# Later adaLN columns as sums along rows of a re-laid w_ada on VectorE, and three empty deferred jobs behind each key block

## The chip, the core and the metric

The kernel runs on one core of one Trainium2 chip. The metric is the device time of one execution in microseconds (us). The kernel before takes 1604.93 us, the median of 3 runs (1604.6 to 1605.01).

The engines are named as in the profile: PE is TensorE's matmul queue and PEld its weight loads, DVE is VectorE, ACT is ScalarE, POOL is GpSimd, SP is SyncE, which issues most of the DMAs. PSUM is the memory that TensorE writes its results to, SBUF the memory that all engines work from.

## What is computed

One trunk layer of a hybrid encoder, for a prompt of 1024 rows and a sample of 32 rows at once (1056 columns in the kernel, which keeps activations transposed, features on partitions). Each of the two has its own condition vector c (1024 values), and all of adaLN comes from it:

```python
mod = jax.nn.silu(c) @ w_ada + b_ada
sh1, sc1, gt1, sh2, sc2, gt2 = jnp.split(mod[:, None, :], 6, axis=-1)

h = rmsnorm(x, g_mix) * (1 + sc1) + sh1
u = h @ w_in
...
x = x + gt1 * (merged @ w_out)
h2 = rmsnorm(x, g_ffn) * (1 + sc2) + sh2
g, up = jnp.split(h2 @ w_gate_up, 2, axis=-1)
x = x + gt2 * ((jax.nn.silu(g) * up) @ w_down)
```

`w_ada` is 1024 x 6144 f32 (D = 1024). `sh1` and `sc1`, its first 2D columns, are needed before anything is projected. The other four vectors, columns 2D to 6D, are needed only after attention and the mLSTM. Between them, `u` is split into queries, keys and values of 8 attention heads (64 wide, in pairs `hp` of 128 partitions), the mLSTM's q, k, v and gates, and the merge gates; band softmax attention and the chunked mLSTM run on them.

## The kernel before

**Matmuls.** f32 products are made of three passes of a high and a low part (`PASSES`). A *unit* (L440) is one PSUM tile of 128 x 352: 8 steps k over the 1024 input features, 3 matmuls of 128x352 each, so 24 matmuls. A block of 128 output columns (a key block, a query block, a gate block) is three units, 72 matmuls. The class `Weights` (L55) loads raw weights ahead through SP (`wraw`, L423) and has ACT and DVE or POOL split them into high and low parts (`wsp`, L413 and L414).

**The order.** PE, ACT, DVE and POOL run in the order in which the program writes their instructions. SP's order is chosen by a scheduler, so an SP DMA can be placed elsewhere than written, but SP too issues in order. Other work is written between the matmuls of a unit by the class `Side` (L102), in two ways:

- *jobs*: generators that are stepped at every `tick` (at odd k, so four per unit), each at its own rate of steps per tick;
- *later*: a list of deferred functions; `flush(1)` takes one from the front at k = 2, 4 and 6 of each unit.

```python
            if k % 2 == 0 and k:
                side.flush(1)
            if k % 2 == 1:
                side.tick()
```

**The start.** `first_ada` (L320) makes `sh1` and `sc1` with TensorE as `w_ada`'s first 2D columns arrive; `first_units` (L471) makes the first key and value blocks of head pair 0 step by step as input rows become ready (L479). The key block (`k_block`, L548) evacuates PSUM with ACT L557 and L560 and DVE L562. The value block (`v_block`, L582) copies the value columns out of PSUM to `vf` with ACT L590 and appends to `later`: `v_tail` for the first four column blocks of 128, an empty job, `v_tail` for the other four, an empty job, and `v_sample`. `v_tail` (L608) transposes four blocks on TensorE (L615) into an `mm` PSUM tile, splits them (ACT L603, DVE L606), and the second one writes tokens out (`put_tokens`, L577, ACT L579). `v_sample` (L620) uses `sample_tail` (L569, TensorE L571, DVE L573). Then comes the query block (`q_block`, L629): three units at L447, evacuated with ACT L643 and L646. The `mm` pool has 3 PSUM buffers.

**Attention** for each of the four head pairs is a job beside the next head pair's projections. Per query block: scores on TensorE (L728) into `psS`; DVE L742 adds the bias and takes the row's extreme; ACT L743 is the exponential with a row sum; DVE L747 and POOL L748 normalise; TensorE L755 transposes into `psT`; ACT L762 copies the high part and DVE L767 makes the low part; TensorE L786 multiplies by the values into `psV`; ACT L792 and DVE L793 and L794 take it out. `psS`, `psT` and `psV` have one buffer each.

**Stretches.** `segs` (L1304) lists them: 0 the first head pair's blocks, 1 to 4 other projections with attention of head pairs 0 to 3 beside, 5 and 6 the mLSTM. At stretch 1 the job `ada_rest` (L1196) starts, 160 steps over 495 ticks, so one step in about three ticks. It computes the four later adaLN vectors without TensorE's weight path. For each of 8 chunks of 512 columns and each of 8 blocks k of 128 rows, a piece of `w_ada` (128 x 512, tile `wa`, 2 buffers, loaded by `ada_load`, L1190, DMA at L1194) is scaled by the column of silu(c) for its rows and added up:

```python
    if k == 0:
        dve.tensor_scalar(ac[:, c], wa, cmix[:, c, 0:1], None, op0=ALU.mult)
    else:
        dve.scalar_tensor_tensor(ac[:, c], wa, cmix[:, c, k:k + 1], ac[:, c],
                                 op0=ALU.mult, op1=ALU.add)
```

These are L1205 (16 times) and L1207 (112 times). The sum over the 128 rows of a block lies across partitions. So for each chunk POOL swaps the halves of the second condition (L1213, L1214), DVE adds (L1216), TensorE transposes four blocks (L1221, 32 in all), DVE reduces along the row (L1224) and adds the bias (L1225). `cmix` is silu(c) with its two conditions swapped between halves of the partitions, made by POOL in `param_cols` (L229).

Of the kernel before, what the change touches and what calls it, by code (L numbers as in the profile page):

```python
# [8 lines left out]
F32 = mybir.dt.float32  # L9
# [130 lines left out]
def hybrid_stream_step(  # L140
# [3 lines left out]
    params, w_ada, w_in, b_if, rel_row, w_br_att, w_br_mlstm, w_out, w_gate_up, w_down, g_final,  # L144
# [82 lines left out]
    cmix = cp.tile([P, 2, KD], F32, name="cmix")  # L227
# [320 lines left out]
    def k_block(hp):  # L548
        w = w_cols(KA + hp * P)

        def run():
            kt = att_k[hp] = slot([P, 2, T], F32R)
            kf = ap_.tile([P, T - 512], F32, tag="kf", name=nm("kf"), bufs=1)
            for lo, hi, pt in units(w):

                for hh, (u, v) in enumerate(ROWS):
                    act.activation(kt[u, hh, lo:hi], pt[u], AF.Copy)  # L557
                a = max(lo, 512)
                if a < hi:
                    act.activation(kf[:, a - 512:hi - 512], pt[:, a - lo:], AF.Copy)  # L560
                for hh, (u, v) in enumerate(ROWS):
                    dve.tensor_tensor(kt[v, hh, lo:hi], pt[u], f(kt[u, hh, lo:hi]), op=ALU.subtract)  # L562
            W.advance()
            sp.dma_start(new_k_p[hp], kf[:, :512])
            sp.dma_start(new_k_s[hp], kf[:, 512:])
        run.w = w
        return run

    def sample_tail(src, out, hp):  # L569
        pt = mmt()  # L570
        pe.transpose(pt[:TS, :P], src, ident)  # L571
# [259 lines left out]
    maskbig = gp.tile([P, P], F32, name="maskbig")  # L831
# [7 lines left out]
    def mlstm_setup():  # L839
        pool.memset(tri, 1.0)  # L840
        pool.affine_select(out=tri, in_=tri, compare_op=ALU.is_ge, fill=0.0, base=0,
                           pattern=[[1, P]], channel_multiplier=-1)
        pool.memset(maskbig, 0.0)
        pool.affine_select(out=maskbig, in_=maskbig, compare_op=ALU.is_ge, fill=BIG, base=0,
# [206 lines left out]
    def mlstm(pr):  # L1051
# [24 lines left out]
        def first(i):  # L1076
# [113 lines left out]
    def ada_load(n):  # L1190
        if n < 8 * KD:
            ch, k = divmod(n, KD)
            wa = ada_tiles[n] = ada_tile()
            sp.dma_start(wa, w_ada[k * P:(k + 1) * P, 2 * D + ch * 512:2 * D + (ch + 1) * 512])  # L1194

    def ada_rest():  # L1196


        for ch in range(8):
            ac = tmpt((P, 2, 512))  # L1200
            for k in range(KD):
                wa = ada_tiles.pop(ch * KD + k)
                for c in range(2):
                    if k == 0:
                        dve.tensor_scalar(ac[:, c], wa, cmix[:, c, 0:1], None, op0=ALU.mult)  # L1205
                    else:
                        dve.scalar_tensor_tensor(ac[:, c], wa, cmix[:, c, k:k + 1], ac[:, c],  # L1207
                                                 op0=ALU.mult, op1=ALU.add)
                    if c == 0:
                        ada_load(ch * KD + k + 1)  # L1210
                    yield
            swapped = ada_tile()
            pool.tensor_scalar(swapped[:DH], ac[DH:, 1], 1.0, 1.0, op0=ALU.mult, op1=ALU.mult)  # L1213
            pool.tensor_scalar(swapped[DH:], ac[:DH, 1], 1.0, 1.0, op0=ALU.mult, op1=ALU.mult)  # L1214
            yield
            dve.tensor_tensor(ac[:, 0], ac[:, 0], swapped, op=ALU.add)  # L1216
            yield
            yield
            pt = mmt()
            for j in range(4):  # L1220
                pe.transpose(pt[:, j * P:(j + 1) * P], ac[:, 0, j * P:(j + 1) * P], ident)  # L1221
            r0 = R_ADA + 2 * KD + ch * 4
            am = amod2[:, ch // 2, :, (ch % 2) * 4:(ch % 2 + 1) * 4]
            dve.tensor_reduce(am, pt.rearrange("p (k c r) -> p c k r", c=2, r=DH), mybir.AxisListType.X, ALU.add)  # L1224
            dve.tensor_tensor(am, am, cols[:, r0:r0 + 4].unsqueeze(1).to_broadcast([P, 2, 4]), op=ALU.add)  # L1225
            yield
# [3 lines left out]
    ADA_STEPS = 160  # L1230
# [61 lines left out]
    def open_mls():  # L1292
# [3 lines left out]
        mp_t.append(mls_cm)  # L1296

# [911 lines left out]
    for j in range(KD):  # L2209
# [30 lines left out]
        "params", "w_ada", "w_in", "b_if", "rel_bias",  # L2240
# [41 lines left out]
```

## Time and profile before

| | |
|---|---|
| median of 3 runs | 1604.93 us |
| the profiled execution | 1605.1 us |
| its span | 1603.4 us |
| TensorE's granted clock | full in nearly all slices of the span |
| DMA moved | 192.45 MB, 120 GB/s on the mean |

The span is the profiled execution from its first to its last instruction, without what lies around it. The profile's 40 slices show TensorE at 90% or more in all but the first two and the last:

```profile
PE   7899999999999999999999999999999999999997
DVE  7766564647776855455654699998888986799754
ACT  3556454544455544443443655544544444545443
```

Each digit is the busy share of one fortieth of the span in tenths. Such a profile is read from the engine that is always busy: the places where it stands still are few, and each has a row among its waits.

### The profile page before, as it was taken

The page shows a single profiled execution, that of the slowest core. Times are in us where ns is not written, and L with a number is a line of the kernel's source. Part 1 is how long each engine was busy: PE and PEld are TensorE (multiplying, and loading weights), DVE is VectorE, ACT ScalarE, POOL GpSimd, SP SyncE. Part 2 cuts the span into 40 slices and gives each one's busy share as a digit, 9 for nine tenths or more (in the row PEclk, how much of TensorE's full clock was granted, in tenths as well). Part 3 has the DMA queues.
Part 4 walks back from the last instruction along what each step waited for, and adds up shares of the span by engine and source line. Part 5 has one row for each costly group of instructions (what it writes and reads, how often), then busy time and mean ns, then how long its engine had stood idle before and what let it go on. Part 6 is the DMA issues. An engine that isn't in the chain of part 4 may idle for free.

```text
span 1603.4 us, 27301 instructions
## 1 busy us (share of the span) xinstructions
PE 1574.2 (98%) x10229; PEld 1554.3 (97%) x10229; DVE 1133.5 (71%) x2178; ACT 784.1 (49%) x1743; POOL 443.0 (28%) x470
## 2 busy tenths in 40 slices
PE   7899999999999999999999999999999999999997
PEld 7899999999999999999999999999999999999997
DVE  7766564647776855455654699998888986799754
ACT  3556454544455544443443655544544444545443
POOL 1334243434332411000012100565565650000001
PEclk9999999999999999999999999999999999999999
DMA  9822323232223332685353311213222227427454
GB/s 364 262 83 91 100 82 102 89 122 87 67 80 80 72 94 68 120 279 165 122 154 112 107 54 50 97 56 104 81 80 94 67 84 251 135 79 250 135 155 127
DMA packets 209362, 192.45 MB, mean 120 GB/s; under 512 B 11450, under 2 KB 179038, under 8 KB 208206
## 3 DMA queue, kind: packets, MB, share of 16 engines
q1 hardware_dynamic: 206670, 188.87, 37.9%
q8 instruction: 81, 1.33, 0.4%
q10 hardware_dynamic: 2528, 1.77, 0.4%
q14 instruction: 51, 0.42, 0.1%
q0 software_dynamic: 32, 0.06, 0.0%
HBM read 152.19 MB, written 41.63 MB: 121 GB/s over the span
## 4 chain that ended last, share of the span: by engine, by line
PE 89%; DMA 4%; DVE 3%; ACT 2%; issue 1%; SPq 0%; POOL 0%; ACTq 0%; DVEq 0%; POOLq 0%
PE mm L447 41%; PE psb L1817 18%; PE mm L1817 10%; PE mm L2220 3%; PE mm L884 3%; PE psb L2220 2%; PE psV L786 2%; PE psb L2063 2%; DMA xres<-s 1%; PE psS L728 1%; DMA s<-in_w_ada_dram 1%; PE psT L755 1%; PE mm L2063 1%; DMA wraw<-in_w_in_dram 1%; DMA s<-in_x_prompt_dram 1%
## 5 line engine op out<-in xcount | busy, mean ns | idle before, releaser
L447 PE MATMUL mm<-s,wsp 128*128 128x352 f32 x4104 | 687.8, 324 | 0.0
L447 PEld LDWEIGHTS mm<-s,wsp 128*128 128x128 f32 x4104 | 657.1, 188 | 1.5 <-issue 0.4
L414 DVE TENSOR_TENSOR wsp<-wraw,wsp 128x512 fp32r<-128x512 f32 (+1 forms) x280 | 234.9, 855 | 120.3 <-ACT wsp L413 118.7
L1817 PE MATMUL psb<-s,wsp 128*128 128x352 f32 x1611 | 271.7, 322 | 1.5 <-DVE wsp L414 0.8
L413 ACT ACTIVATE wsp<-wraw 128x512 fp32r<-128x512 f32 x336 | 199.4, 617 | 140.7 <-PE psb L1817 45.5
L1817 PEld LDWEIGHTS psb<-s,wsp 128*128 128x128 f32 x1611 | 260.5, 188 | 2.1 <-DVE wsp L414 1.1
L1817 PE MATMUL mm<-s,wsp 128*128 128x352 f32 x933 | 159.3, 322 | 0.0
L1817 PEld LDWEIGHTS mm<-s,wsp 128*128 128x128 f32 x933 | 151.2, 188 | 0.5 <-DVE wsp L414 0.5
L748 POOL TENSOR_SCALAR st<-st,mx 128x640 f32<-128x640 f32 (+5 forms) x72 | 56.1, 779 | 182.6 <-DVE mx L747 168.3
L1207 DVE SCALAR_TENSOR_TENSOR t<-wa,cmix,t 128x512 f32<-128x512 f32 x112 | 89.8, 807 | 14.3 <-DMA wa<-in_w_ada_dram 14.0
L414 POOL TENSOR_TENSOR wsp<-wraw,wsp 128x512 fp32r<-128x512 f32 x56 | 75.1, 1362 | 50.8 <-ACT wsp L413 50.3
L743 ACT ACTIVATE st<-st,mx 128x640 f32<-128x640 f32 (+5 forms) x72 | 47.9, 665 | 67.3 <-DVE mx L742 67.2
L742 DVE CUSTOM_DVE_ANT_0 st<-psS,bias 128x640 f32<-128x640 f32 (+5 forms) x72 | 44.4, 617 | 49.4 <-PE psS L728 35.2
L762 ACT ACTIVATE pT<-psT 128x640 fp32r<-128x640 f32 (+3 forms) x80 | 38.7, 494 | 64.6 <-PE psT L755 51.2
L1764 POOL TENSOR_TENSOR t<-t,sl 128x352 f32<-128x352 f32 x19 | 18.4, 969 | 182.9 <-ACT sl L1762 182.9
L2132 POOL TENSOR_TENSOR fst<-fst 128x1 f32<-128x1 f32 (+1 forms) x6 | 1.2, 194 | 236.6 <-ACT t L2125 236.6
L767 DVE TENSOR_TENSOR pT<-psT,pT 128x640 fp32r<-128x640 f32 (+3 forms) x80 | 44.0, 558 | 22.3 <-ACT pT L762 22.2
L1426 POOL TENSOR_TENSOR wraw<-wraw,raw 128x512 f32<-128x512 f32 x33 | 55.8, 1704 | 0.9
L884 PE MATMUL mm<-s,s 128*128 128x264 f32 (+3 forms) x432 | 54.7, 283 | 0.0
L2220 PE MATMUL mm<-s,wsp 128*128 128x352 f32 x330 | 54.4, 324 | 0.0
L2220 PEld LDWEIGHTS mm<-s,wsp 128*128 128x128 f32 x330 | 53.1, 188 | 0.0
L1426 POOL TENSOR_TENSOR spare<-wraw 128x512 f32<-128x512 f32 x11 | 16.8, 1527 | 130.0 <-DMA wraw<-in_w_gate_up_dram 122.2
(374 smaller groups left out, 2548.0 us busy)
## 6 DMA issues: line engine op xcount, KB each, us to landing
wraw<-in_w_in_dram SPq DMA_DIRECT2D x38, 512.0 KB, 4.3
wraw<-in_w_gate_up_dram SPq DMA_DIRECT2D x33, 512.0 KB, 4.0
wa<-in_w_ada_dram SPq DMA_DIRECT2D x64, 256.0 KB, 2.8
wraw<-in_w_down_dram SPq DMA_DIRECT2D x32, 512.0 KB, 3.7
a_d<-t SPq DMA_DIRECT2D x22, 528.0 KB, 2.7
g_d<-t SPq DMA_DIRECT2D x16, 528.0 KB, 2.7
x<-xres SPq DMA_DIRECT2D x16, 528.0 KB, 6.5
t<-g_d SPq DMA_DIRECT2D x16, 528.0 KB, 4.6
```

The source lines that it names most:

```text
L413: act.activation(dst[:, 0], src, AF.Copy)
L414: eng.tensor_tensor(dst[:, 1], src, f(dst[:, 0]), op=ALU.subtract)
L447: pe.matmul(pt[:, :hi - lo], wt[(w0 + k) // 4][:, a, (w0 + k) % 4], xt[k][:, b, lo:hi], start=(k == 0 and q == 0), stop=(k == n - 1 and q ...
L742: dve.tensor_tensor_reduce(so, sv, bi, -1.0, 3.0e38, ALU.add, ALU.min, mx[:n, 1:2])
L743: act.activation(st[:n, :w], st[:n, :w], AF.Exp, bias=mx[:n, 1:2], scale=-1.0, accum_out=mx[:n, 2:3])
L748: pool.tensor_scalar(st[:n, :w], st[:n, :w], mx[:n, 3:4], 1.0, op0=ALU.mult, op1=ALU.mult)
L884: pe.matmul(pt[:n, :wd], hs[k][:, a, i * P:i * P + n], whl[b][:, k, :wd], start=(k == 0 and q == 0), stop=(k == KD - 1 and q == 2))
L1207: dve.scalar_tensor_tensor(ac[:, c], wa, cmix[:, c, k:k + 1], ac[:, c], op0=ALU.mult, op1=ALU.add)
L1426: self.eng.tensor_tensor(a(dst), a(x), a(y), op=op)
L1817: pe.matmul(acc, wt[:, a, k], x[k][:, b], start=(start and not onto and k == 0 and q == 0), stop=(stop and k == 3 and q == 2), skip_group_ ...
L2063: pe.matmul(acc, wt[k // 4][:, u, k % 4], piece_of[k, i][:, v], start=(k == 0 and q == 0), stop=(k == KP - 1 and q == 2))
L2220: pe.matmul(acc, wt[(k - k0) // 4][:, u, (k - k0) % 4], piece_of[k, 2][:, v], start=(k == 0 and q == 0), stop=(k == NF - 1 and q == 2))
```

## The change

**Later adaLN columns.** The host lays columns 2D to 6D of `w_ada` out as `w_mod`: two halves of the 1024 rows, 32 blocks of 128 columns, and in each a piece of 128 columns (on partitions) by 512 rows. `ada_rest` loads, for each half, 512 values of both conditions onto all partitions (`crow`), takes ACT's Silu of them (128 x 1024), and then makes one DVE instruction per piece and condition, 128 in all: it multiplies the piece by the row of silu(c) and sums along the row, into one column of `sums`. The products themselves go to a bf16 tile that nobody reads (`junk`). At the end the two halves and the bias are added. The swaps on POOL, the transposes on TensorE, the reductions and `cmix` are gone. It takes 138 steps over the same 495 ticks. `w_ada` keeps only its first 2D columns, so their pieces lie contiguous.

**Three empty jobs.** Each key block appends three empty functions to `later`.

**Tiles.** `sample_tail` has a staging tile of its own, `put_tokens` one buffer in place of two, and the mask of the mLSTM (`maskbig`) moves to the pool that opens with stretch 5.

```diff
     def param_cols():
         act.activation(csil, cols[:, R_C:R_C + 16].rearrange("p (c k) -> p k c", c=2), AF.Silu)
-        for c in range(2):
-            pool.tensor_copy(cmix[:DH, c], csil[:DH, :, c])
-            pool.tensor_copy(cmix[DH:, c], csil[DH:, :, 1 - c])
...
             sp.dma_start(new_k_s[hp], kf[:, 512:])
+            side.later += [lambda: None] * 3
...
-        stg = ap_.tile([P, 4, P], F32, tag="stg", name=nm("stg"), bufs=2)
-        dve.tensor_copy(stg[:TS, 0], pt[:TS, :P])
+        stg = ap_.tile([TS, P], F32, tag="stgs", name=nm("stg"), bufs=1)
+        dve.tensor_copy(stg, pt[:TS, :P])
...
     def put_tokens(pt, out, hp):
-        stg = ap_.tile([P, 4, P], F32, tag="stg", name=nm("stg"), bufs=2)
+        stg = ap_.tile([P, 4, P], F32, tag="stg", name=nm("stg"), bufs=1)
...
     def ada_load(n):
-        if n < 8 * KD:
-            ch, k = divmod(n, KD)
+        if n < 64:
+            half, b = divmod(n, 32)
             wa = ada_tiles[n] = ada_tile()
-            sp.dma_start(wa, w_ada[k * P:(k + 1) * P, 2 * D + ch * 512:2 * D + (ch + 1) * 512])
+            sp.dma_start(wa, w_mod[half, b])

     def ada_rest():
-        for ch in range(8):
-            ac = tmpt((P, 2, 512))
-            for k in range(KD):
-                wa = ada_tiles.pop(ch * KD + k)
+        junk = gp.tile([P, 512], BF16, tag="junk", name="junk", bufs=1)
+        sums = gp.tile([P, 2, 4, 2, KD], F32, tag="sums", name="sums", bufs=1)
+        for half in range(2):
+            crow = tmpt((P, 2, 512))
+            c0 = c_rows[:, half * 512:(half + 1) * 512]
+            sp.dma_start(crow, bass.AP(c0.tensor, c0.offset, [[0, P], [D, 2], [1, 512]]))
+            for _ in range(3):
+                yield
+            act.activation(crow, crow, AF.Silu)
+            yield
+            for b in range(32):
+                wa = ada_tiles.pop(half * 32 + b)
                 for c in range(2):
-                    if k == 0:
-                        dve.tensor_scalar(ac[:, c], wa, cmix[:, c, 0:1], None, op0=ALU.mult)
-                    else:
-                        dve.scalar_tensor_tensor(ac[:, c], wa, cmix[:, c, k:k + 1], ac[:, c],
-                                                 op0=ALU.mult, op1=ALU.add)
+                    at = sums[:, half, b // KD, c, b % KD:b % KD + 1]
+                    dve.tensor_tensor_reduce(junk, wa, crow[:, c], 1.0, 0.0, ALU.mult, ALU.add, at)
                     if c == 0:
-                        ada_load(ch * KD + k + 1)
+                        ada_load(half * 32 + b + 1)
                     yield
-            swapped = ada_tile()
-            pool.tensor_scalar(swapped[:DH], ac[DH:, 1], 1.0, 1.0, op0=ALU.mult, op1=ALU.mult)
-            pool.tensor_scalar(swapped[DH:], ac[:DH, 1], 1.0, 1.0, op0=ALU.mult, op1=ALU.mult)
-            yield
-            dve.tensor_tensor(ac[:, 0], ac[:, 0], swapped, op=ALU.add)
-            yield
-            yield
-            pt = mmt()
-            for j in range(4):
-                pe.transpose(pt[:, j * P:(j + 1) * P], ac[:, 0, j * P:(j + 1) * P], ident)
...
+        dve.tensor_tensor(amod2, sums[:, 0], sums[:, 1], op=ALU.add)
+        r0 = R_ADA + 2 * KD
+        bias = cols[:, r0:r0 + 4 * KD].rearrange("p (v j) -> p v j", v=4)
+        for c in range(2):
+            dve.tensor_tensor(amod2[:, :, c], amod2[:, :, c], bias, op=ALU.add)
...
-    ADA_STEPS = 160
+    ADA_STEPS = 138
...
+        elif name == "c_rows":
+            a = _np.concatenate([_np.asarray(inputs["c_prompt"]), _np.asarray(inputs["c_sample"])])
+        elif name == "w_mod":
+            a = _np.asarray(inputs["w_ada"])[0, :, 2 * D:].reshape(2, 512, 4 * KD, P).transpose(0, 2, 3, 1)
...
+        if name == "w_ada":
+            a = a[:, :, :2 * D]
```

**Where instructions move.** Lines of the changed kernel are 3 to 6 lower than before, up to the job itself. On TensorE, the first two units of head pair 0's query block before: `mm_729` is unit 1, `mm_779` unit 2, the rows with `ident` are the value transposes.

```order
L447 MATMUL mm_729<-s_520,s_637 128x352 x3
L615 MATMUL mm_740<-ident,t_714 128x128 x4
L447 MATMUL mm_729<-s_547,s_637 128x352 x3
L447 MATMUL mm_729<-s_574,s_637 128x352 x3
L447 MATMUL mm_729<-s_600,s_637 128x352 x3
L447 MATMUL mm_729<-s_627,s_637 128x352 x3
L615 MATMUL mm_759<-ident,t_714 128x128 x4
L447 MATMUL mm_729<-s_664,s_637 128x352 x3
L447 MATMUL mm_779<-s_438,s_637 128x352 x3
```

The same place in the changed kernel: `mm_723` is unit 1, `mm_755` unit 2.

```order
L443 MATMUL mm_723<-s_621,s_631 128x352 x3
L443 MATMUL mm_723<-s_658,s_631 128x352 x3
L443 MATMUL mm_755<-s_432,s_631 128x352 x3
L443 MATMUL mm_755<-s_480,s_631 128x352 x3
L443 MATMUL mm_755<-s_514,s_631 128x352 x3
L612 MATMUL mm_766<-ident,t_708 128x128 x4
L443 MATMUL mm_755<-s_541,s_631 128x352 x3
L443 MATMUL mm_755<-s_568,s_631 128x352 x3
L443 MATMUL mm_755<-s_594,s_631 128x352 x3
L443 MATMUL mm_755<-s_621,s_631 128x352 x3
L612 MATMUL mm_785<-ident,t_708 128x128 x4
```

Both groups of value transposes moved from unit 1 to unit 2, 24 matmuls later. For later head pairs the three empty jobs are used up by flushes that had nothing to do, and TensorE's order stays.

On ACT, early in the first attention, before (`pT` rows are L762, `st` rows the exponentials, `t_914` takes `psV` out):

```order
L762 ACTIVATE pT_1022<-psT_1021 128x256
L743 ACTIVATE st_1027,mx_1028<-st_1027,mx_1028 128x512
L762 ACTIVATE pT_1060<-psT_1059 128x384
L743 ACTIVATE st_1066,mx_1067<-st_1066,mx_1067 128x640
L792 ACTIVATE t_914<-psV_1036 64x256
```

And in the changed kernel:

```order
L759 ACTIVATE pT_1011<-psT_1010 128x256
L740 ACTIVATE st_1016,mx_1017<-st_1016,mx_1017 128x512
L1201 ACT_TABLE_LOAD
L1201 ACTIVATE t_889<-t_889 128x1024
L759 ACTIVATE pT_1047<-psT_1046 128x384
L740 ACT_TABLE_LOAD
L740 ACTIVATE st_1053,mx_1054<-st_1053,mx_1054 128x640
L789 ACTIVATE t_908<-psV_1025 64x256
```

A table load and the Silu of `crow` (`t_889`) stand behind the exponential of 512 columns, and a second table load ahead of the next exponential. The same three instructions stand once more in the fourth attention, between a copy of L1022 and the `pT` of 384 columns.

On DVE at the same place, before (`t_893` is the old job's accumulator):

```order
L562 TENSOR_TENSOR s_858<-mm_955,s_858 64x352 x2
L1207 SCALAR_TENSOR_TENSOR t_893<-wa_895,cmix,t_893 128x512
L742 ISA st_1027,mx_1028<-psS_1026,bias_915 128x512
L742 ISA mx_1028 128x1
L767 TENSOR_TENSOR pT_1022<-psT_1021,pT_1022 128x256
L747 RECIPROCAL mx_1028<-mx_1028 128x1
L1207 SCALAR_TENSOR_TENSOR t_893<-wa_969,cmix,t_893 128x512
```

And in the changed kernel:

```order
L558 TENSOR_TENSOR s_852<-mm_948,s_852 64x352 x2
L739 ISA st_1016,mx_1017<-psS_1015,bias_909 128x512
L739 ISA mx_1017 128x1
L764 TENSOR_TENSOR pT_1011<-psT_1010,pT_1011 128x256
L744 RECIPROCAL mx_1017<-mx_1017 128x1
L739 ISA st_1053,mx_1054<-psS_1052,bias_909 128x640
L739 ISA mx_1054 128x1
L764 TENSOR_TENSOR pT_1047<-psT_1046,pT_1047 128x384
L744 RECIPROCAL mx_1054<-mx_1054 128x1
L790 TENSOR_TENSOR t_908<-psV_1025,t_908 64x256
L791 TENSOR_TENSOR t_908<-psV_1025,t_908 64x256
L1207 ISA junk,sums<-wa_718,t_889 128x512
```

The old job's instructions between the attention's own are gone here; the first of the new sums (L1207 of the changed kernel) comes behind the next two query blocks' work. From there on one sum stands about where one product stood, each with a read of its accumulator. On SP the load of `crow` is placed right behind the first `wa` piece.

More of the change, by code (lines that the diff above doesn't have):

```diff
@@ L143, in hybrid_stream_step @@
     x_prompt, x_sample, cache_k, cache_v, state_conv, state_C, state_n, state_m,
-    params, w_ada, w_in, b_if, rel_row, w_br_att, w_br_mlstm, w_out, w_gate_up, w_down, g_final,
+    params, c_rows, w_ada, w_mod, w_in, b_if, rel_row, w_br_att, w_br_mlstm, w_out, w_gate_up, w_down, g_final,
     y_prompt, y_sample, new_k_p, new_v_p, new_conv_p, new_C_p, new_n_p, new_m_p,
@@ L226, in hybrid_stream_step @@
     csil = cp.tile([P, KD, 2], F32, name="csil")
-    cmix = cp.tile([P, 2, KD], F32, name="cmix")
     def param_cols():
         act.activation(csil, cols[:, R_C:R_C + 16].rearrange("p (c k) -> p k c", c=2), AF.Silu)
-        for c in range(2):
-            pool.tensor_copy(cmix[:DH, c], csil[:DH, :, c])
-            pool.tensor_copy(cmix[DH:, c], csil[DH:, :, 1 - c])
     def bc2(ap):
@@ L571, in sample_tail @@
         pe.transpose(pt[:TS, :P], src, ident)
-        stg = ap_.tile([P, 4, P], F32, tag="stg", name=nm("stg"), bufs=2)
-        dve.tensor_copy(stg[:TS, 0], pt[:TS, :P])
-        sp.dma_start(out[0, 0].rearrange("t h d -> t (h d)")[:, hp * P:(hp + 1) * P], stg[:TS, 0])
-        return stg[:TS, 0]
+        stg = ap_.tile([TS, P], F32, tag="stgs", name=nm("stg"), bufs=1)
+        dve.tensor_copy(stg, pt[:TS, :P])
+        sp.dma_start(out[0, 0].rearrange("t h d -> t (h d)")[:, hp * P:(hp + 1) * P], stg)
+        return stg
     def put_tokens(pt, out, hp):
-        stg = ap_.tile([P, 4, P], F32, tag="stg", name=nm("stg"), bufs=2)
+        stg = ap_.tile([P, 4, P], F32, tag="stg", name=nm("stg"), bufs=1)
         act.activation(stg, pt.rearrange("p (i c) -> p i c", i=4), AF.Copy)
@@ L830, in hybrid_stream_step @@
     tri = gp.tile([P, P], F32, name="tri")
-    maskbig = gp.tile([P, P], F32, name="maskbig")
+    masks = []
     vm = [None, None]
@@ L841, in mlstm_setup @@
         pool.affine_select(out=tri, in_=tri, compare_op=ALU.is_ge, fill=0.0, base=0,
-                           pattern=[[1, P]], channel_multiplier=-1)
-        pool.memset(maskbig, 0.0)
-        pool.affine_select(out=maskbig, in_=maskbig, compare_op=ALU.is_ge, fill=BIG, base=0,
                            pattern=[[1, P]], channel_multiplier=-1)
@@ L1090, in first @@
                 r = r0 + hh
-                dve.scalar_tensor_tensor(Wt[:n, hh, :n], mb[:n, hh, :n], gw[:n, 5, r:r + 1], maskbig[:n, :n],
+                dve.scalar_tensor_tensor(Wt[:n, hh, :n], mb[:n, hh, :n], gw[:n, 5, r:r + 1], masks[0][:n, :n],
                                          op0=ALU.subtract, op1=ALU.max)
@@ L1219, in ada_rest @@
-            pt = mmt()
-            for j in range(4):
[L1221 to L1226, printed above, removed]
+        dve.tensor_tensor(amod2, sums[:, 0], sums[:, 1], op=ALU.add)
@@ L1296, in open_mls @@
         mp_t.append(mls_cm)
+        maskbig = mp_t[0].tile([P, P], F32, tag="maskbig", name="maskbig", bufs=1)
+        pool.memset(maskbig, 0.0)
+        pool.affine_select(out=maskbig, in_=maskbig, compare_op=ALU.is_ge, fill=BIG, base=0,
+                           pattern=[[1, P]], channel_multiplier=-1)
+        masks.append(maskbig)
     def conv_rows():
@@ L2239 @@
 _INS = ["x_prompt", "x_sample", "cache_k", "cache_v", "state_conv", "state_C", "state_n", "state_m",
-        "params", "w_ada", "w_in", "b_if", "rel_bias",
+        "params", "c_rows", "w_ada", "w_mod", "w_in", "b_if", "rel_bias",
         "w_br_att", "w_br_mlstm", "w_out", "w_gate_up", "w_down", "g_final"]
```

## Prediction

> **What bounds the kernel now.** I read the page first, then TensorE's waits, then stretches of the timeline where the changed instructions stand.
>
> ```profile
> span 1603.4 us, 27301 instructions
> PE 1574.2 (98%) x10229; PEld 1554.3 (97%) x10229; DVE 1133.5 (71%) x2178; ACT 784.1 (49%) x1743; POOL 443.0 (28%) x470
> ```
>
> TensorE (PE) is busy for 1574.2 of 1603.4 us; VectorE (DVE) has 29% to spare, ScalarE (ACT) half, GpSimd (POOL) most. So a microsecond counts only if TensorE works or stands in it, and everything is priced there. The profiled execution took 1605.1 us, 1.7 more than its span and 0.2 over the median of 1604.93; sums are made against 1605.1.
>
> TensorE's longest waits by what they waited for (total, times, longest) are few:
>
> ```profile
> PE mm L615 <- ACT t L590: 3.1, 1, 3.1
> PE psT L755 <- POOL wsp L414: 1.5, 1, 1.5
> PE psT L755 <- DVE pT L767: 1.0, 1, 1.0
> ```
>
> The change touches the surroundings of all three.
>
> **Part a: the transposes that go.** TensorE's timeline at one of the eight chunks of the old job (start, length, instruction, count):
>
> ```profile
> 172.25 1.28 PE L447 MATMUL mm<-s,wsp 128*128 128x352 f32 x7
> 173.37 0.60 PE L1221 MATMUL mm<-ident,t 128*128 128x128 f32 x4
> 173.73 1.04 PE L447 MATMUL mm<-s,wsp 128*128 128x352 f32 x5
> ```
>
> One matmul takes 0.32 us from start to end, and seven span 1.28, so they start (1.28 - 0.32) / 6 = 0.16 us apart. The four transposes begin at 173.37 and the next matmul at 173.73: 0.36 us inserted. The five behind them span 1.04 where 4 x 0.16 + 0.32 = 0.96 was due: 0.08 more. So 0.44 us a chunk, and 8 chunks give **-3.5 us**. No wait goes with it: TensorE stood for none of these transposes.
>
> **Part b: the wait ahead of the value transposes.** ACT and PE as the first query block begins:
>
> ```profile
> 68.37 1.69 PE L447 MATMUL mm<-s,s 128*128 128x352 f32 x9
> ...
> 72.61 0.80 ACT L590 ACTIVATE t<-psS 128x352 f32<-128x352 f32 x2
> 73.11 1.12 PE L615 MATMUL mm<-ident,t 128*128 128x128 f32 x4 [3.06 <-ACT t L590]
> 73.30 0.47 ACT L590 ACTIVATE t<-psT 128x352 f32<-128x352 f32 x1
> ...
> 76.82 0.60 PE L615 MATMUL mm<-ident,t 128*128 128x128 f32 x4
> 77.17 3.16 PE L447 MATMUL mm<-s,s 128*128 128x352 f32 x18
> ...
> 80.73 0.46 ACT L643 ACTIVATE t<-mm 128x352 f32<-128x352 f32 x1 [1.32 <-PE mm L571]
> 82.07 2.19 PE L447 MATMUL mm<-s,s 128*128 128x352 f32 x12 [0.16 <-ACT s L646]
> ```
>
> After nine matmuls TensorE meets the transposes of the values (L615), whose source ACT copies out of PSUM (L590) only at 72.6: 3.06 us of idle. Three empty jobs ahead in the list take unit 1's three flushes, so the transposes come a unit of 24 matmuls later: unit 1 runs through to 68.37 + 24 x 0.16 = 72.2, the transposes are due nine matmuls on, at 73.7, and L590's last copy ends at 73.77, of which the first transposes use the first two. The wait goes.
>
> It had a second price. This window shows 2.9 us from its end (length, PE, PEld, DVE, ACT, POOL, then the granted TensorE clock, DMA share, GB/s):
>
> ```profile
> 73.10:76.00 2.90, 2.89 (x11) 2.83 (x12) 0.69 (x1) 1.26 (x3) 2.80 (x4) 0.51 0.17 55
> ```
>
> The clock was 0.51, so 2.9 us did the work of 1.5: 1.4 lost. Together 4.5 us.
>
> [...]
>
> What is late next: ACT must have freed unit 2's PSUM buffer before the next key block starts. Today the second transposes end at 77.42 and that evacuation (L643, L646) at 82.0, with a store's issue and the token copy between: 4.6 us. Then, the second transposes end at 73.7 + 0.44 + 12 x 0.16 + 0.36 = 76.4, so the buffer is free at 81.0; TensorE arrives at 72.2 + 48 x 0.16 + two groups of 0.44 + one small transpose, 81.0. I allow a wait of 0.1: **-4.4 us**.
>
> **Part c: a stall that VectorE made.** Early in the first attention:
>
> ```profile
> 102.39 1.32 DVE L1207 SCALAR_TENSOR_TENSOR t<-wa,cmix,t 128x512 f32<-128x512 f32 x1
> 103.74 0.69 DVE L742 CUSTOM_DVE_ANT_0 st<-psS,bias 128x512 f32<-128x512 f32 x1
> 104.36 0.42 DVE L767 TENSOR_TENSOR pT<-psT,pT 128x256 fp32r<-128x256 f32 x1
> 104.47 0.72 ACT L743 ACTIVATE st<-st,mx 128x512 f32<-128x512 f32 x1 [1.89 <-DVE mx L742]
> 104.92 0.52 PE L755 MATMUL psT<-ident,st 128*128 128x128 f32 x3 [1.47 <-POOL wsp L414]
> ```
>
> The profile names POOL, but there is one psT buffer, and L767, its last reader, ends at 104.78, just before TensorE starts. L767 stood behind an old product (L1207, 1.32 us). The new sums start later than this, so nothing stands there: **-1.2 us** of the 1.47, bounds 0 and -1.5.
>
> **Part d: ScalarE's two detours.** Each half now has a Silu on 128x1024 between exponentials, with a table load ahead of it and one behind. None stands there today; the nearest rows by form:
>
> ```profile
> L1033 ACT ACTIVATE s<-t,cols 128x1024 f32<-128x1024 f32 x8 | 9.9, 1234 | 0.0
> L743 ACT ACT_TABLE_LOAD x1 | 1.3, 1283 | 0.0
> ```
>
> So 1.28 + 1.23 + 1.28 = 3.8 us of ACT each time. TensorE pays between 0 (hidden) and 3.8. The first detour stands behind the exponential of 104.47, ahead of these:
>
> ```profile
> 105.54 0.49 ACT L762 ACTIVATE pT<-psT 128x384 fp32r<-128x384 f32 x1 [0.25 <-PE psT L755]
> ...
> 107.04 0.83 ACT L743 ACTIVATE st<-st,mx 128x640 f32<-128x640 f32 x1 [1.01 <-DVE mx L742]
> ...
> 108.03 0.60 PE L755 MATMUL psT<-ident,st 128*128 128x128 f32 x4
> ...
> 108.85 0.42 DVE L794 TENSOR_TENSOR t<-psV,t 64x256 f32<-64x256 f32 x1
> ...
> 109.41 0.59 PE L786 MATMUL psV<-pT,s 128*128 128x256 f32 x3 [0.20 <-ACT pT L762]
> ```
>
> I walk it on today's clock. ACT is free at 105.3, the accumulator read; table to 106.6, Silu to 107.8, pT 128x384 to 108.3, its low part on VectorE (0.42 for 256 columns above, some 0.55 here) to 108.9: the next L755 waits 0.9 for psT. Second table to 109.6, exponential and what reads psV behind it: today L794 ends 2.23 us after that exponential starts, so at 111.8. L786, due at 109.2 + 0.9, waits 1.7 for the one psV buffer, today 0.2: +1.5. Together +2.4.
>
> The second detour, in the fourth attention:
>
> ```profile
> 419.59 0.45 ACT L1022 ACTIVATE t<-mm 128x352 f32<-128x352 f32 x1
> ...
> 422.48 0.83 ACT L743 ACTIVATE st<-st,mx 128x640 f32<-128x640 f32 x1 [1.07 <-DVE mx L742]
> ...
> 424.29 0.42 DVE L794 TENSOR_TENSOR t<-psV,t 64x256 f32<-64x256 f32 x1
> 424.74 0.75 DVE L1207 SCALAR_TENSOR_TENSOR t<-wa,cmix,t 128x512 f32<-128x512 f32 x1
> ...
> 431.00 0.74 PE L755 MATMUL psT<-ident,st 128*128 128x128 f32 x5 [0.96 <-DVE pT L767]
> ```
>
> It stands behind L1022. ACT: 420.04 + 2.5 (table, Silu) + 0.5 (pT) + 1.3 (table) = 424.3, so the exponential is 1.8 late, and so is L794; VectorE then has one old product (0.75) fewer on its way to the L767 for which TensorE waits at 431.0. That is 1.1 later, and the wait at 431.0 grows by 1.1. **d = +2.4 + 1.1 = +3.5 us**, bounds 0 and 7.6.
>
> **Part e: what costs nothing.** VectorE's old job and the nearest rows for a new sum:
>
> ```profile
> L1207 DVE SCALAR_TENSOR_TENSOR t<-wa,cmix,t 128x512 f32<-128x512 f32 x112 | 89.8, 807 | 14.3 <-DMA wa<-in_w_ada_dram 14.0
> L742 DVE CUSTOM_DVE_ANT_0 st<-psS,bias 128x512 f32<-128x512 f32 x8 | 5.5, 691 | 4.4 <-PE psS L728 3.1 <-POOL wsp L414 1.3
> L277 DVE CUSTOM_DVE_ANT_0 t<-s 128x1024 bf16<-128x1024 f32 x8 | 9.7, 1224 | 5.7 <-DMA s<-in_x_prompt_dram 5.6
> ```
>
> A sum with its result is the form of L742 and L277, multiply or add and reduce in one pass. 512 columns take 0.69, so 128 sums take 88 us and about 10 more for reading accumulators: about as much as 112 x 0.807 plus the starts and reductions now. Upper bound 1.22 each, the row for 1024 columns. I take 0.69, since L277 itself, from SBUF, comes to 0.61 per 512. POOL loses copies that it had time for. The copied row of c is issued where the first w_ada piece is today, well ahead of the first attention's Silu: 0. The mask and the single staging buffer stay behind other work on POOL and ACT: 0; uncovered, each is one instruction, under 1 us. The first adaLN columns now come in contiguous pieces. Windows of the loads of x (contiguous, first row) and of w_ada (second), columns as above:
>
> ```profile
> 4.00:8.00 4.00, 2.66 (x12) 2.40 (x13) 3.12 (x5) 1.02 (x2) 0.00 (x0) 1.00 1.03 416
> 18.00:22.00 4.00, 3.62 (x30) 3.22 (x29) 2.97 (x4) 1.67 (x11) 2.29 (x2) 1.00 1.03 426
> ```
>
> Both fill the DMA engines (1.03) at 416 and 426 GB/s, so nothing is gained: 0, bounds -1 and +1.
>
> **Sum:** 1605.1 - 3.5 - 4.4 - 1.2 + 3.5 = 1599.5 us.
>
> **Rivals.**
> 1. *The detours are hidden and the VectorE waits go whole:* -3.5 - 4.5 - 1.5 - 1.0 = -10.5, 1594.6. For it: ACT is 49% busy. Against: psT and psV are single.
> 2. *The later place does not remove the wait:* TensorE now waits for ACT at the next key block, where I found no slack; b goes to 0: 1603.9. For it: the 0.16 at 82.07. Against: that is all it is today.
> 3. *Both detours fall on TensorE whole:* 7.6 for 3.5, 1603.6.
> 4. *A sum takes 1.22 us:* 128 x 1.3 = 166 us of VectorE for 115, half a microsecond more ahead of L767 each time; three waits like the 1.0 above make +3: 1602.5. [...]
> 5. *Slower: late sums hold SyncE's queue.* SyncE issues in order, and a w_ada load waits for the sum that frees its buffer, with weight loads behind it:
>
> ```profile
> SPq L1194 <- DVE t L1207: 108.9, 34, 9.2
> ```
>
> Its longest hold, 9.2 us, passes unseen today. It decides from about two blocks of weights, 2 x 72 matmuls x 0.16 = 23 us; then TensorE would idle as in b, 4.5 us a time, and three such holds give 1599.5 + 13.5 = 1613.
>
> **How the numbers follow.** Forecast 0.61 (1599.5, own range 1597 to 1602), rival 1 0.16, rivals 2, 3 and 4 0.06 each, rival 5 0.05. The range runs from 1594 to 1603: it takes in the forecast, rivals 1 and 4, and leaves out 0.17. A difference of 0.2%, 3.2 us, is about what measurement can tell from no change, so faster means below 1601.7: 0.58 + 0.16 = 0.74. Same: the rest of the forecast and rivals 2 to 4, 0.21. Slower: 0.05.
>
> **What would show it.** a: no four-transpose groups in the attention stretches. b: no wait of L615 (now some lines lower), clock 1.00 at 73 to 76 us. c: the 1.5 gone. d: two rows of Silu 128x1024, 3.8 us between the neighbours on ACT, and TensorE's waits at psT and psV behind each, 2.4 and 1.1 more. e: sums of 0.69. A sum far longer, a wait at the second key block, or SyncE holds over 20 us would make the forecast wrong.

## The result and the profile after

The changed kernel takes 1601.13 us (median of 14 runs, 1600.18 to 1603.17) against 1604.72 us for the kernel before in the same comparison: the ratio is 0.9979, 95% interval 0.9971 to 0.9987. That is 3.6 us faster, where 5.6 were forecast, and inside the range. The profiled execution took 1600.87 us, 4.2 less than the profiled one of before; its span is 4.9 shorter.

The head of the page of the changed kernel, and TensorE's waits there (total, times, longest):

```profile
span 1598.5 us, 27336 instructions
PE 1569.2 (98%) x10197; PEld 1549.3 (97%) x10197; DVE 1122.9 (70%) x2285; ACT 791.3 (50%) x1749; POOL 423.3 (26%) x450
```
```profile
PE psT L752 <- DVE pT L764: 2.5, 3, 2.0
PE psV L783 <- ACT pT L759: 2.0, 2, 1.7
...
PE psS L725 <- DVE mx L739: 0.6, 1, 0.6
```

The wait of L615 and the one put down to POOL are gone. The one for L767 (now L764) has grown from 1.0 to 2.5 us and the one at psV for L762 (now L759) from 0.4 to 2.0, and the one at psS is new. TensorE has 32 instructions fewer and is busy 5.0 us less. The starts of the same TensorE instruction in the two traces give the path of the gain (worked out from both traces, us from the span's start):

```
TensorE instruction                        before    after    difference
first matmul of the first query unit        68.37    68.87      +0.50
first matmul of the second key block        86.02    81.52      -4.50
scores, 256 columns                         93.94    90.22      -3.72
transposes, 384 columns                    104.92    99.52      -5.40
transposes, 512 columns                    108.03   103.06      -4.97
values of three blocks                     109.41   106.00      -3.41
scores behind the first old chunk          177.64   173.80      -3.84
ahead of the second detour                 406.70   401.65      -5.05
transposes behind the second detour        431.00   426.97      -4.03
behind the seventh old chunk               627.90   622.60      -5.30
last instruction                                                -5.10
```

The terms of the prediction stand in this table as steps of the last column. The first row, 0.5 us at the start, comes before anything that was forecast to matter; a second profile of before (below) has its first query unit at 68.97, so the start varies by that much on its own.

**The value transposes.** TensorE, and then the copies of L590 (now L587), in the changed kernel:

```profile
68.87 5.55 PE L443 MATMUL mm<-s,s 128*128 128x352 f32 x33
74.25 0.60 PE L612 MATMUL mm<-ident,t 128*128 128x128 f32 x4
74.61 2.19 PE L443 MATMUL mm<-s,s 128*128 128x352 f32 x12
76.64 0.60 PE L612 MATMUL mm<-ident,t 128*128 128x128 f32 x4
76.99 3.12 PE L443 MATMUL mm<-s,s 128*128 128x352 f32 x18
```
```profile
72.65 0.47 ACT L587 ACTIVATE t<-psT 128x352 f32<-128x352 f32 x1
72.99 0.47 ACT L640 ACTIVATE t<-mm 128x352 f32<-128x352 f32 x1
73.35 0.93 ACT L643 ACTIVATE s<-mm 64x352 fp32r<-64x352 f32 x2
```

33 matmuls run without a break, and the copies are done a microsecond before the transposes. Unit 1's evacuation (L640, L643) now comes ahead of the token work and not behind it. The window that held 11 matmuls at a clock of 0.51 holds 22 at 1.00:

```profile
73.10:76.00 2.90, 2.90 (x22) 2.88 (x21) 1.72 (x3) 1.75 (x5) 2.80 (x3) 1.00 0.24 49
```

**The first detour.** ACT, DVE and PE behind the first Silu, in order of time:

```profile
99.58 1.28 ACT L1201 ACT_TABLE_LOAD   x1
...
100.88 1.06 ACT L1201 ACTIVATE t<-t 128x1024 f32<-128x1024 f32 x1
...
101.84 0.48 ACT L759 ACTIVATE pT<-psT 128x384 fp32r<-128x384 f32 x1
102.34 1.28 ACT L740 ACT_TABLE_LOAD   x1
102.35 0.56 DVE L764 TENSOR_TENSOR pT<-psT,pT 128x384 fp32r<-128x384 f32 x1 [0.78 <-ACT pT L759]
103.06 0.63 PE L752 MATMUL psT<-ident,st 128*128 128x128 f32 x4 [0.29 <-DVE pT L764]
...
103.63 0.83 ACT L740 ACTIVATE st<-st,mx 128x640 f32<-128x640 f32 x1
...
105.44 0.42 DVE L791 TENSOR_TENSOR t<-psV,t 64x256 f32<-64x256 f32 x1
...
106.00 0.59 PE L783 MATMUL psV<-pT,s 128*128 128x256 f32 x3 [1.73 <-ACT pT L759]
```

Read it downwards: table, Silu, pT, table, exponential, and the two TensorE waits where they were forecast, 0.29 for psT and 1.73 for psV, whose last reader L791 ends at 105.86. The profile names L759; L791 is what ends just before. In the second detour the wait of 0.96 at 431.0 has become this one, forecast at 2.1:

```profile
426.97 0.74 PE L752 MATMUL psT<-ident,st 128*128 128x128 f32 x5 [1.98 <-DVE pT L764]
```

### The profile page after: what moved, and what is told of

It reads as the page before. It is cut to its first block, busy times and chain, and to the rows that moved or that the text cites. A ratio compares the mean times of both kernels' runs of the same rounds, so it can differ in the third digit from the quotient of the medians.

```text
span 1598.5 us, 27336 instructions
## 1 busy us (share of the span) xinstructions
PE 1569.2 (98%) x10197; PEld 1549.3 (97%) x10197; DVE 1122.9 (70%) x2285; ACT 791.3 (50%) x1749; POOL 423.3 (26%) x450
## 4 chain that ended last, share of the span: by engine, by line
PE 91%; DVE 3%; DMA 2%; ACT 2%; issue 1%; SPq 0%; POOL 0%; ACTq 0%; DVEq 0%; POOLq 0%
PE mm L443 41%; PE psb L1811 18%; PE mm L1811 10%; PE mm L2214 3%; PE mm L878 3%; PE psb L2214 2%; PE psV L783 2%; PE psb L2057 2%; PE psS L725 2%; DMA s<-in_w_ada_dram 1%; PE psT L752 1%; PE mm L2057 1%; DMA t<-in_x_sample_dram 1%; PE psV L1112 1%; PE mm L475 1%
## 5 line engine op out<-in xcount | busy, mean ns | idle before, releaser
L1207 DVE CUSTOM_DVE_ANT_0 junk<-wa,t 128x512 bf16<-128x512 f32 x128 | 94.9, 742 | 2.8 <-DMA wa<-in_w_mod_dram 1.8
L759 ACT ACTIVATE pT<-psT 128x640 fp32r<-128x640 f32 (+3 forms) x80 | 38.7, 493 | 62.6 <-PE psT L752 47.5
L764 DVE TENSOR_TENSOR pT<-psT,pT 128x640 fp32r<-128x640 f32 (+3 forms) x80 | 44.0, 558 | 22.2 <-ACT pT L759 22.2
L878 PEld LDWEIGHTS mm<-s,s 128*128 128x128 f32 (+1 forms) x432 | 52.0, 179 | 0.5
```

Source lines behind the costliest of these rows:

```text
L878: pe.matmul(pt[:n, :wd], hs[k][:, a, i * P:i * P + n], whl[b][:, k, :wd], start=(k == 0 and q == 0), stop=(k == KD - 1 and q == 2))
L1207: dve.tensor_tensor_reduce(junk, wa, crow[:, c], 1.0, 0.0, ALU.mult, ALU.add, at)
```

## The experiments

The comparisons ran on several chips, on which the kernel before took 1604.0 to 1604.7 us; each number below is set against before of its own comparison.

**One part alone: the empty jobs.** The kernel before with one line more:

```diff
             sp.dma_start(new_k_s[hp], kf[:, 512:])
+            side.later += [lambda: None] * 3
```

> The kernel before with the three empty jobs alone. My theory: the wait at the value transposes and the half clock behind it go (4.5 us), 0.8 us comes back where the first attention's scores wait for VectorE, and the stall of 1.5 us behind the old product stays: 3.7 to 4.5 us under the kernel before, about 1600.7. No row of a wait at L615, granted clock 1.00 from 73 to 76 us. Rival (the wait only moves to the next key block): within 1 us of the kernel before. If the spread of the changed kernel's runs (1600.2 to 1603.2) comes from ScalarE's detours, the runs here stand close together, as those of before do.

1602.6 against 1604.3 us, ratio 0.9988 (0.9979 to 0.9997): 1.7 us, less than half of what I expected. The profiled execution was the longest of the 11. The stretch from the first query unit to the second key block is as short as in the changed kernel (12.66 us; 12.65 there). Then 1.3 us are lost where the scores wait, and 0.4 at the next transposes; in this execution 0.8 more goes near 1475 us, behind a wait of 0.6 us for VectorE. VectorE and TensorE of this kernel:

```profile
86.68 2.15 DVE L628 TENSOR_TENSOR s<-t,s 64x352 fp32r<-64x352 f32 x2
...
88.86 0.49 DVE L1206 TENSOR_SCALAR t<-wa,cmix 128x512 f32<-128x512 f32 x1
89.38 1.06 DVE L562 TENSOR_TENSOR s<-mm,s 64x352 fp32r<-64x352 f32 x2
90.47 0.29 DVE L743 CUSTOM_DVE_ANT_0 st<-psS,bias 128x128 f32<-128x128 f32 x1
...
90.83 0.51 PE L729 MATMUL psS<-s,s 128*128 128x256 f32 x2 [1.12 <-DVE mx L743]
```

TensorE arrives four microseconds earlier and meets a VectorE that is still in its row of old work. The first old product (L1206, 0.49 us) is part of that row; in the changed kernel it is not there, and the wait is 0.62 in place of 1.12. So the two halves of the change help each other: the late start of the sums saves part of what the jobs gain.

**One part alone: the sums.** The changed kernel without the line above.

> The changed kernel without the three empty jobs. My theory: transposes gone -3.4, the VectorE stall -1.5, the two detours +3.0, so about 2 us under the kernel before, 1602.8; the wait of some 3 us at the value transposes is back, with half clock behind it. Rival (the new sums are what gains, the jobs do nothing): as the changed kernel, 1601.

1604.23 against 1604.3 us, ratio 1.0001 (0.9992 to 1.001): no change that can be measured, where I expected 2 us. In the profile the terms are there as steps (transposes 0.4 a chunk, VectorE's stall -1.6, the detours +2.0 and +1.0), and TensorE ends 1.1 us earlier than in the profile of before. The wait at the value transposes, which I expected at some 3 us with half clock behind it, is 1.4 us here, and the mean granted clock of the execution is 0.998, where the profiled one of before has 0.997; the third query unit waits 2.9 us for ScalarE instead, a place that is priced further down. Over all runs, the median span is 0.6 us under that of before, and the median time around the span 0.5 us longer (2.2 for 1.7), so nothing is left. The runs go from 1602.65 to 1606.55 us; where such a spread comes from is shown below.

**The table loads.** One word of the changed kernel:

```diff
-            act.activation(crow, crow, AF.Silu)
+            act.activation(crow, crow, AF.Exp)
```

> The changed kernel with an exponential where the later adaLN columns take Silu of c, so that these columns hold other values. ScalarE then loads no tables there: a detour is one activation of 1.06 us where it was 3.63. My theory (TensorE's waits behind the detours are made by the table loads): the waits of 0.3 and 1.7 us after 103 us and the growth of the one at 427 us go, 2 to 3 us under the changed kernel, about 1598.3; and its runs no longer spread to 1603, if that spread is half clock that these waits bring on. Rival (VectorE's order or the Silu itself makes them wait): within 0.7 us of the changed kernel.

1597.01 us, ratio 0.9956 (0.9942 to 0.997), 7.3 us under before, and the runs lie between 1596.16 and 1597.49. The table of starts no longer has the detours' steps; at the second place the wait even falls by 0.6, as one old product is gone from VectorE. An activation of 1.05 us in the same place costs TensorE nothing. The price was the two loads of 1.28 us around the Silu.

**No second Silu.** silu(c) stands in SBUF as columns from the start on.

```diff
+    sc_d = dr.tile([2, D], F32, name="sc_d")
...
                 ada_load(0)
+                for c in range(2):
+                    sp.dma_start(sc_d[c].rearrange("(k p) -> p k", p=P), csil[:, :, c])
...
-            c0 = c_rows[:, half * 512:(half + 1) * 512]
+            c0 = sc_d[:, half * 512:(half + 1) * 512]
...
-            for _ in range(3):
+            for _ in range(4):
                 yield
-            act.activation(crow, crow, AF.Silu)
-            yield
```

> The changed kernel, but silu(c) is not computed a second time: the columns that the start computes are written to a row in DRAM (2048 numbers of 4 bytes) and that row is copied onto all partitions. ScalarE has no detour at all. My theory: as with an exponential in its place or 0.3 us better, about 1598, no spread. Rival: the small writes hold SyncE's queue ahead of the bias loads and the first scores wait for them: no better than the changed kernel, with a wait of TensorE or VectorE near 90 us for a DMA.

1599.94 us, ratio 0.9971 (0.996 to 0.9983): between the two theories, and the rival's place is visible. Of this kernel, SyncE, VectorE and TensorE:

```profile
89.31 0.37 SPq L1201 DMA_DIRECT2D t<-sc_d  x1
...
91.32 0.29 DVE L742 CUSTOM_DVE_ANT_0 st<-psS,bias 128x128 f32<-128x128 f32 x1 [1.43 <-POOL bias L695]
...
91.68 0.71 PE L728 MATMUL psS<-s,s 128*128 128x256 f32 x2 [2.24 <-DVE mx L742]
```

The read of the row waits until 89.3 us, and the first bias tile arrives late; TensorE stands 2.24 us. Behind that wait the clock was at half for the whole of this window of 3.2 us:

```profile
91.90:95.10 3.20, 3.20 (x12) 3.20 (x12) 1.03 (x5) 2.09 (x7) 0.85 (x2) 0.50 0.91 271
```

**The same by a transpose.** One transpose of the columns on TensorE in place of the second empty job, a copy, and one store of 16 rows. The rows are read back with two DMAs a half, and the Silu of `crow` is gone as in e4:

```diff
-            side.later += [lambda: None] * 3
+            side.later += [lambda: None, silu_rows if hp == 0 else lambda: None, lambda: None]
...
+    def silu_rows():
+        pt = mmt()
+        pe.transpose(pt[:2 * KD, :P], csil.rearrange("p k c -> p (k c)"), ident)
+        stg = ap_.tile([TS, P], F32, tag="stgs", name=nm("stg"), bufs=1)
+        dve.tensor_copy(stg[:2 * KD], pt[:2 * KD, :P])
+        sp.dma_start(sc_d, stg[:2 * KD])
```

> As e4, but the rows of silu(c) get to DRAM by one transpose on TensorE (16 rows of 128, in place of the second empty job), a copy on VectorE and one store of 8 KB. My theory: what e4 lost was the 2048 small writes (SyncE's read of them waited until 89.3 us, and the bias with it); so the wait of 2.2 us for VectorE at 91.7 goes back to about 0.7 and no detour is left: 0.2 to 0.5 us above e3, because of one transpose and one more copy, about 1597.3. Rival (what e4 lost against e3 is not the writes): about 1600, as e4.

1596.88 us (1596.6 to 1597.03) against 1604.41, ratio 0.9954 (0.9941 to 0.9966): 7.5 us under before, about twice the gain of the change as made, and the same as e3 in its comparison (0.9956). It computes all that the changed kernel does, and is the best version found. The waits at psT and psV are back at 0.4 and 0.3 at most, and the one at the scores is 0.5.

**The cache's split behind the first scores.** As e7, with the jobs put this way; attention takes the cache's tiles only when it reads them, which this order needs:

```diff
-                side.later.append(lambda: cache_kv(ckv))
+                side.later += [lambda: None] * 9 + [lambda: cache_kv(ckv)]
```

> As e7, with the split of the cached keys and values nine flushes later, behind the first scores. My theory: the first scores' wait for VectorE (0.6 us in the changed kernel, 1.1 in e1, both with the split of the cache ahead of them on VectorE) goes: 0.5 to 0.8 us under e7. Rival (the work only moves into the next query blocks' way): no gain, a wait of TensorE for L764 or L739 between 95 and 100 us.

1597.73 us, 0.85 above e7 and with no run under e7's slowest: the rival. The scores' wait is gone, and a larger one stands ten microseconds later, behind the moved copies:

```profile
97.53 0.69 DVE L611 TENSOR_TENSOR s<-t,s 128x512 fp32r<-128x512 f32 x1
98.24 1.06 DVE L559 TENSOR_TENSOR s<-mm,s 64x352 fp32r<-64x352 f32 x2
...
99.33 0.69 DVE L746 CUSTOM_DVE_ANT_0 st<-psS,bias 128x512 f32<-128x512 f32 x1
...
100.51 0.52 PE L759 MATMUL psT<-ident,st 128*128 128x128 f32 x3 [1.49 <-DVE pT L771]
```

**Sums twice.** Each `tensor_tensor_reduce` of the changed kernel stands twice.

> The changed kernel with each new sum issued twice, so 256 in place of 128, some 98 us more of VectorE; the values stay the same. My theory (the sums are off the path): within 1 us of the changed kernel, 1600.5 to 1602. Rival (VectorE is close to the bound in the attention stretches, or SyncE's queue is held longer): 5 us or more above it, with new waits of TensorE for L764 or L739.

1614.24 us, ratio 1.0062 (1.0048 to 1.0076): 13 us above the changed kernel, and my expectation missed by an order of magnitude. Against the starts in before, the loss comes in steps of 0.3 to 1.8 us at 17 places from 125 to 550 us. The stretch of the attentions, the changed kernel in the first row and the one with doubled sums in the second (columns as before: length, PE, PEld, DVE):

```profile
105.00:450.00 345.00, 340.74 (x2325) 331.97 (x2326) 205.63 (x593) 178.47 (x409) 121.04 (x159) 1.00 0.30 90
```
```profile
105.00:450.00 345.00, 333.48 (x2250) 322.83 (x2251) 258.82 (x710) 168.96 (x394) 125.29 (x154) 1.00 0.28 88
```

VectorE was busy 60% of that stretch and has 25% to spare even with the sums doubled; TensorE falls back all the same, by 75 matmuls. Its waits with doubled sums, of which the changed kernel has 2.5 and 0.6 us:

```profile
PE psT L752 <- DVE pT L764: 5.9, 6, 2.7
...
PE psS L725 <- DVE mx L739: 1.7, 2, 1.1
```

Each extra sum stands in VectorE's order ahead of the attention's next instructions, which have to free psT and psS, of one buffer each. SyncE's holds for the pieces add up to 209 us in both kernels, so that part of the rival did not come. VectorE's idle share is therefore no slack for work put in anywhere. The mean granted clock of this execution is 0.997, where the changed kernel's profiled one has 0.998, so a part of its loss may be half clock; which part was not shown.

**The kernel before, profiled again.**

> The kernel before once more, with a profile. The profile shown had 3.4 us of half clock behind the wait at the value transposes; its span was 1603.4 us, and most spans of this kernel in the comparisons since are 1602.0 to 1602.7. My theory: the half clock comes in some executions only, so a window of 73 to 76 us now shows a granted clock of 1.00 and a span near 1602.3. Rival: the half clock is there each time (0.5 in that window) and the difference in span comes from somewhere else.

The clock is 1.00 at 73 to 76 us as expected, but the span is 1603.2, not 1602.3. Why both profiled executions of before are longer than most of its others stays open. TensorE of this second profile of before:

```profile
72.49 0.79 PE L615 MATMUL mm<-ident,t 128*128 128x128 f32 x4 [1.84 <-ACT t L590]
...
81.81 2.51 PE L447 MATMUL mm<-s,s 128*128 128x352 f32 x14 [1.67 <-ACT s L646]
```

Without the half clock and with a shorter wait at L615, the third query unit still starts at 81.81 (82.07 in the profile shown): it waits for L646. So the half clock was real, but it stood beside something longer.

**The token store by SyncE.**

> The kernel before, with the store of the value tokens issued by SyncE in place of ScalarE. In two profiles of before, ScalarE stood at that store's issue until 80.0 and 80.2 us, and the evacuation of the query block's first unit behind it freed its PSUM buffer at about 82; TensorE's third unit started at 81.8 and 82.1 whether the clock had been at half before or not. My theory: the stretch from the first query unit to the second key block costs 17.7 and 16.8 us because of that issue behind the value transposes, not because of the half clock; without it the third unit starts 1.5 us earlier in an execution without half clock, and the median falls by 1 to 1.7 us. Rival (the half clock and the wait at L615 are the whole cost): within 0.4 us of the kernel before.

```diff
     def put_tokens(pt, out, hp):
...
-        act.dma_start(
+        sp.dma_start(
```

1602.38 against 1604.0 us, ratio 0.9992 (0.9983 to 1.0001). The interval just takes in 1, so the times alone do not settle it; the medians are 1.6 us apart as expected, and the profile shows the place. ScalarE and TensorE of this kernel:

```profile
77.03 0.46 ACT L643 ACTIVATE t<-mm 128x352 f32<-128x352 f32 x1
```
```profile
72.00 0.79 PE L615 MATMUL mm<-ident,t 128*128 128x128 f32 x4 [1.60 <-ACT t L590]
...
77.93 5.56 PE L447 MATMUL mm<-s,s 128*128 128x352 f32 x33
```

The evacuation of unit 1 starts at 77.03 and no longer at 80.5 to 80.7, and the third unit runs on without a wait. The stretch from the first query unit to the second key block takes 14.6 us, where it takes 16.8 in the second profile of before, which has no half clock (1.00 from 73.1 to 92 us). In the kernel before, ScalarE stood at the issue of the token store until 80.0 or 80.2 us with that evacuation behind it. What held the store's issue itself, no row says; in the two profiles of before it began 0.8 and 2.3 us behind the copy that it stores, in the changed kernel 0.1.

**The changed kernel, profiled again.**

> The changed kernel once more, with a profile. Its spans are 1598.3 us in about half of the runs and 1599.5 to 1600.8 in the rest, at a granted clock of 0.996 or 0.997; e3 and e7, without the waits behind the detours, keep within 0.9 and 0.5 us. My theory: in the longer runs a window of half clock of 3.4 us follows TensorE's waits behind the first detour (103 to 107 us). If this execution is a longer one, the clock between 103 and 110 us reads under 1.00. Rival: the half clock lies at the first scores (90 us) or at the start, before 69 us.

A short one: 1598.2. With the next it makes the pair.

> The same as look_after_1: about 4 chances in 10 that this execution is a longer one. If its span is 1598.3 the clock stays 1.00 from 20 us to the end's last microseconds.

A longer one: 1599.9. The same window of the two, short first:

```profile
105.80:109.20 3.40, 3.20 (x21) 3.23 (x22) 2.17 (x7) 1.52 (x4) 0.68 (x1) 1.00 0.02 5
```
```profile
105.80:109.20 3.40, 3.40 (x13) 3.40 (x14) 1.93 (x6) 0.92 (x2) 0.81 (x1) 0.50 0.02 5
```

The waits of both are alike (1.7 us at psV, to 106.0 and 105.8); in the longer one half clock follows, 13 matmuls are done in place of 21, and the difference of 1.7 us stays to the end. That fits the spread of the changed kernel: seven of its 14 spans are 1598.3 to 1598.7, seven 1599.5 to 1600.8, though only one of the longer kind was profiled. e2 has the same detours and spreads more; e3 and e7 have no table loads there and spread by 0.9 and 0.5 us.

**The form of w_ada.** The slice of the first 2D columns on the host is left out.

```diff
-        if name == "w_ada":
-            a = a[:, :, :2 * D]
```

> The changed kernel with w_ada given whole again, so that its first 2D columns are read in pieces of 8 KB a row out of rows of 24 KB, as in the kernel before. My theory (the form of the piece makes no difference to the start): within 0.5 us of the changed kernel, and TensorE's waits for w_ada at 2 to 3.5 us in total. Rival (contiguous pieces make it worse, since these waits were 2.1 and 2.4 us in two profiles of the kernel before and 2.7 to 3.5 in most of those with cut pieces): 0.5 to 1 us under the changed kernel.

1602.21 against 1604.32 us, ratio 0.9985 (0.9975 to 0.9994). The median lies 1.1 us above the changed kernel's, which neither the theory nor the rival expected, but the two intervals overlap, and ten of the 11 spans are of the longer kind; its profile has the half clock from 105.8 to 109.2 too. The waits for w_ada add up to 3.2 us. Nothing here speaks for a gain or a loss by the form of the piece; how often the half clock comes would have to be told apart first.

## Why the prediction was right, and where it was off

**a, -3.5:** right. The differences step at each of the eight old chunks, by 0.43 to 0.45, and 3.5 in all.

**b, -4.4:** near in the number, in part by luck, and half right in the mechanism. L615's wait went, and the stretch to the second key block shortened by 5.0 us against the profile shown and by 4.1 against the second one (17.66 and 16.79 to 12.65). But the 3.06 + 1.4 of which I made the term was the wrong pair: without half clock and with 1.84 of wait, before loses nearly as much, since ScalarE's store issue kept unit 1's buffer. By the 14.6 us of e9, about half of the 4.1 belongs to the store's issue and half to the wait at L615. The three empty jobs remove both, because they also put unit 1's evacuation ahead of the token work on ScalarE; the prediction did not see that. The number came near because the wait with the half clock and the chain over the store's issue end at the same place, the third unit. Nor was "what is late next" ScalarE with 0.1 us: the runs showed VectorE at the first scores, 0.62 us of wait and a step of 0.8, which leaves -4.2. Rival 2's wait for ScalarE at the next key block did not come.

**c, -1.2:** -1.7 in the table, the whole stall. L767 stood behind the old product, as said.

**d, +3.5:** +3.0, that is 2.0 (2.4 forecast) and 1.0 (1.1). The Silu took 1.06 us and not 1.23. Each load took the 1.28 us of the forecast, and the next instruction starts 0.02 and 0.01 us behind it (at 100.88 and 103.63 in the rows above), so ScalarE lost no more than the loads themselves.

**e, nothing:** the swap of 128 old instructions for 128 new cost nothing that the table shows; a sum took 0.68 us at the median, where 0.69 was forecast, and 0.74 on the mean, in the groups of the changed kernel:

```profile
L1207 DVE CUSTOM_DVE_ANT_0 junk<-wa,t 128x512 bf16<-128x512 f32 x128 | 94.9, 742 | 2.8 <-DMA wa<-in_w_mod_dram 1.8
```

Rival 4, 1.22 us a sum, did not come. But that VectorE has 29% to spare, as the prediction begins, is not why: e5 priced a further 128 sums at 13 us. That the first 128 were free because they took the places of others fits both kernels; it is argued, not shown by a run of its own.

**The sum:** the forecast time was 1.6 us low. TensorE's path gained 5.1 where 5.6 were summed, and that they are so near is luck in part. The four terms came to -6.4 (-3.5, -4.2, -1.7, +3.0), 0.8 more than forecast; the start, ahead of all that was changed, took 0.5 back, and some 0.8 came back in small steps, 0.3 of it near 720 us, for which no row gives a cause. The span gained 4.9, and the profiled time 4.2, since the time around the span grew: 1605.1 less 1603.4 is 1.7, 1600.87 less 1598.5 is 2.4. In the 14 runs it is about 1.9 or 2.3; e7, which reads no rows of c, has 1.7 to 1.9, and e4, which reads none either, 2.0. What takes it stays open. The median lies 0.3 above the profiled run, as half of the executions are of the longer kind, by all that the profiles show with half clock behind the first detour. This was the term that the prediction lacked: in the longer execution that was profiled, waits of 2.0 us behind the first detour cost 3.7, of which 1.7 is the half clock.

Rival 1, hidden detours, did not come, for the reason given against it, single psT and psV. e3 and e7 show what it would have been worth. SyncE's holds for the new pieces reached 14.9 us, where the old ones reached 9.2, and did no harm that the waits of TensorE show.

## What to carry to other kernels

Beside an engine that runs in order behind single PSUM buffers, price a small piece of work by whom it stands ahead of, and not by the engine's idle share: here 1.05 us of ScalarE was free, 3.6 us cost 2 in one place and 1 in another, and another 104 us of sums (198.8 in place of 94.9) on an engine 60% busy cost 13. Before a second activation function is put between others, see if its result exists already in another layout; one transpose and a store of 8 KB took the place of four table loads. And where a wait is removed, look for the whole chain that ends at the same place: take a second profile of the same kernel, since a wait and a half clock that differ between two executions with the same end are not all that sets it.

## What the hardware showed

The half clock did not come after a fixed length of waiting. In the profile of before shown, the granted clock is 0.91 from 69.9 to 73.1 us, 0.51 from 73.1 to 76.0 and 1.00 from 76.0 to 82.0, which makes some 3.4 us of half clock; in look_after_2 it is 0.50 from 105.8 to 109.2, and in e4 from 91.9 to 95.1. It stood beside a wait of TensorE of 3.06 us in that profile of before, and not beside one of 1.84 in the second (1.00 from 73.1 to 92 us); beside one of 2.24 in e4; and beside the 1.7 at psV in look_after_2, but not beside the same wait in two other executions of the same program (1.00 from 105.8 to 109.2 us in the profile shown and in look_after_1).
